# Merge, memory-query and output products of block 2: pairs of column tiles made by Strassen's seven products of quarters

## The chip, the cores and the metric

The kernel runs as one program on one core of a Trainium2 chip. The metric is the device time of one execution in microseconds; the kernel before was timed in three runs. The engines are TensorE (PE, with its weight loads shown as PEld), VectorE (DVE), ScalarE (ACT), GpSimd (POOL) and SyncE (SP, which issues the DMAs).

## The reference

Two blocks of two layers each on 512 tokens of 1024 features, in float32. Block 1 (16 extra tokens in front) mixes windowed attention and an mLSTM. Block 2's layer is the one that the change touches:

```python
h = rmsnorm(x, g_norm)
z = einsum('bsd,dn->bsn', h, w_in)          # 13312 columns, split as
dq, dk, dv, dg, lq, lk, lv, lg, mq, mg, mgate = split(z)
y_a = (rmsnorm(diff_attention(dq, dk, dv)) * (1 - lam_init) * silu(dg)) @ w_br_diff
y_b = (dilated attention of three groups (lq, lk, lv) * silu(lg)) @ w_br_dil
y_m = (memory_attention(mq, keys, values of mem) * silu(mg)) @ w_br_mem
merged = sum over 3 branches of sigmoid(mgate[i]) * (y_a, y_b, y_m)[i]
x = x + merged @ w_out
```

## The kernel before

Activations lie with features on the 128 partitions and the 512 tokens along the free axis: eight tiles of 128 features are one operand. Float32 accuracy is had from three passes: each operand is split into a high and a low part, both float32r (`split`, lines 170 to 174: ACT casts the high part, DVE subtracts it from the source), and `dense` (line 189) adds high·high, high·low and low·high. One dense product of 1024 features by 128 columns is thus 24 matmuls of 512 columns, all into one PSUM bank.

Weights come by DMA in chunks of 128 × 1024 words on SP's queue (`weights`, line 176; tiles `wr`, two buffers), and are split into `wh` and `wl` (three buffers each); of every third chunk POOL makes the low part (line 184), of the others DVE (line 171).

A layer of block 2 (`layer2`) goes in this order: 8 differential heads, 4 dilated heads, then keys and values of the memory (`mem_kv`), 4 memory heads (a dense product for the query and one for the gate each), the merge, and the output projection. The merge has two parts: in part 0 each of 8 column tiles gets one gate product and one product with `w_br_diff`; in part 1 two gate products and two half products with `w_br_dil` and `w_br_mem`. `proj` (line 1206) evacuates a product with a multiplication by the token's norm. Line 1301 makes tanh of a gate, line 1308 multiplies by it, line 1310 (POOL) adds to the sum `acc`, which is then split by line 174. The output projection is eight dense products; line 1327 adds the residual, and `nxt` prepares the next layer's input (parts on lines 173 and 174, squares on 254 and 255).

Attention work is written as generators that move on by a stage whenever `step` is called after a dense product, so that its instructions stand between the products. Intermediate tiles are taken first in, first out from 70 slots in SBUF; a slot's next writer waits for its last reader. The final order on each engine is made by the framework's list scheduler when the program is built; each engine then works through its own list in order. The evacuation of a product is given 300 instructions of precedence (`AHEAD`).

## Time and profile before

| | |
|---|---|
| timed runs, median of 3 | 2871.14 us (2870.21 to 2872.12) |
| the profiled execution: span from first to last instruction | 2868.8 us |
| PE busy in it | 2776.6 us, 97% |
| DVE, ACT, POOL busy | 68%, 49%, 25% |
| mean granted TensorE clock | 0.989 of 2.4 GHz |

The page shows one execution; its 2868.8 us are 2.3 us below the runs' median, so a sum made in its trace carries over to the runs by adding about that. Busy time of an instruction includes the time in which it has started and is held up. PE's durations overlap (a matmul's row is longer than its distance from the next), so PE's pace is read from starts.

### The profile page before, as it was taken

Reading aid. Unit: us, or ns where it says so; the run is one execution under the profiler, and the core shown is the slowest. Engines: PE = TensorE matmul, PEld = TensorE weight load, DVE = VectorE, ACT = ScalarE, POOL = GpSimd, SP = SyncE. Lnnn points to the kernel's source line nnn. Section 1 sums busy time; section 2 is a strip of 40 time slices with the busy share of each in tenths; the row PEclk is TensorE's granted clock in tenths of the full one; section 3 lists DMA queues with packets and bytes.
Section 4 is the critical chain, followed back from the end, with each engine's and each line's share of the span. In section 5 each row is a group of like instructions: output and inputs, shape, how many; then the busy total and the mean of one; then the engine's idle time right before and its main releaser. Section 6 shows DMA issues by size and latency. Waiting matters only on the chain.

```text
span 2868.8 us, 43625 instructions
## 1 busy us (share of the span) xinstructions
PE 2776.6 (97%) x16728; PEld 2446.4 (85%) x16728; DVE 1964.4 (68%) x4261; ACT 1398.6 (49%) x2649; POOL 728.2 (25%) x610
## 2 busy tenths in 40 slices
PE   7999999999999999999999999999998999999997
PEld 7999989999998878878898888888887888888886
DVE  6999886589889757778555772445777664674344
ACT  5555654556565445556443452234555543453223
POOL 5143322224323232221211211322221121211222
PEclk9999999999999999999999999999999999999998
DMA  3221213311111342222223312243221222322232
GB/s 133 67 67 60 67 54 106 116 67 67 61 66 67 113 133 87 80 72 86 89 68 100 122 67 96 99 137 109 80 79 65 87 88 77 110 91 79 96 125 74
DMA packets 96911, 251.60 MB, mean 88 GB/s; under 512 B 9374, under 2 KB 33638, under 8 KB 96574
## 3 DMA queue, kind: packets, MB, share of 16 engines
q1 hardware_dynamic: 96702, 248.82, 26.3%
q8 instruction: 131, 2.15, 0.3%
q14 instruction: 78, 0.64, 0.1%
HBM read 240.19 MB, written 8.60 MB: 87 GB/s over the span
## 4 chain that ended last, share of the span: by engine, by line
PE 75%; DVE 17%; ACT 4%; issue 2%; DMA 1%; SPq 0%; POOL 0%; DVEq 0%; ACTq 0%; POOLq 0%
PE z L164 54%; PE a L164 18%; DVE s L171 2%; DVE wl L171 2%; PE a L943 1%; PE a L486 1%; DVE s L413 1%; DVE s L458 1%; DVE s L329 1%; DVE s L174 1%; DVE s L478 1%; DVE s L276 1%; DVE s L957 1%; DVE s L990 1%; ACT s L470 1%
## 5 line engine op out<-in xcount | busy, mean ns | idle before, releaser
L164 PE MATMUL z<-s,wh 128*128 128x512 f32 (+2 forms) x6784 | 1268.7, 335 | 25.9 <-ACT s L173 9.7
L164 PEld LDWEIGHTS z<-s,wh 128*128 128x128 f32 x6784 | 1045.9, 190 | 159.9 <-ACT s L173 10.3
L164 PE MATMUL z<-s,wl 128*128 128x264 f32 (+2 forms) x3392 | 661.8, 333 | 0.0
L184 POOL TENSOR_TENSOR wl<-wr,wh 128x1024 fp32r<-128x1024 f32 x135 | 333.6, 2471 | 1246.9 <-PE z L164 623.7
L164 PEld LDWEIGHTS z<-s,wl 128*128 128x128 f32 x3392 | 526.5, 188 | 62.4
L170 ACT CAST wh<-wr 128x1024 fp32r<-128x1024 f32 x269 | 281.7, 1048 | 425.5 <-PE z L164 277.8
L164 PE MATMUL a<-s,s 128*128 128x512 f32 (+5 forms) x1900 | 426.6, 339 | 13.9 <-DVE t L458 8.0
L171 DVE TENSOR_TENSOR wl<-wr,wh 128x1024 fp32r<-128x1024 f32 x269 | 354.7, 1321 | 36.9 <-ACT wh L170 32.7
L164 PEld LDWEIGHTS a<-s,s 128*128 128x128 f32 (+1 forms) x1900 | 298.9, 188 | 50.8 <-DVE t L458 9.1
L1206 DVE TENSOR_TENSOR s<-z,s 128x512 f32<-128x512 f32 x128 | 88.0, 688 | 239.9 <-PE z L164 230.3
L183 ACT CAST wh<-wr 128x1024 fp32r<-128x1024 f32 x135 | 141.4, 1048 | 205.0 <-PE z L164 97.1
L171 DVE TENSOR_TENSOR s<-s,s 128x512 fp32r<-128x512 f32 (+6 forms) x272 | 211.7, 789 | 27.4 <-ACT s L170 24.4
L170 ACT CAST s<-s 128x512 fp32r<-128x512 f32 (+6 forms) x272 | 151.1, 567 | 140.3 <-DVE s L1208 26.5
L164 PE MATMUL z<-wh,s 128*128 128x256 f32 x1408 | 208.1, 286 | 5.4 <-DVE s L174 5.0
L164 PEld LDWEIGHTS z<-wh,s 128*128 128x128 f32 x1408 | 188.2, 192 | 14.5 <-DVE s L174 8.1
L171 DVE TENSOR_TENSOR s<-a,s 128x512 fp32r<-128x512 f32 (+3 forms) x266 | 149.8, 581 | 61.2 <-ACT s L170 60.2
L164 PE MATMUL a<-s,wh 128*128 128x512 f32 x768 | 188.2, 393 | 0.0
L170 ACT CAST s<-a 128x512 fp32r<-128x512 f32 (+3 forms) x266 | 127.2, 504 | 93.2 <-PE a L943 49.9
L164 PEld LDWEIGHTS a<-s,wh 128*128 128x128 f32 x768 | 144.0, 188 | 33.4
L957 DVE CUSTOM_DVE_ANT_0 s<-a,reg 128x512 f32<-128x512 f32 x160 | 107.4, 684 | 31.4 <-PE a L164 30.2
L986 ACT ACTIVATE s<-s,t 128x512 f32<-128x512 f32 x128 | 91.3, 715 | 56.7 <-DVE t L983 51.9
L164 PE MATMUL z<-wl,s 128*128 128x256 f32 x704 | 116.9, 284 | 0.0
(254 smaller groups left out, 3068.8 us busy)
## 6 DMA issues: line engine op xcount, KB each, us to landing
wr<-w SPq DMA_DIRECT2D x308, 512.0 KB, 3.5
wr<-wo SPq DMA_DIRECT2D x48, 512.0 KB, 3.4
wr<-wb SPq DMA_DIRECT2D x32, 512.0 KB, 3.5
reg<-tab SPq DMA_DIRECT2D x24, 448.0 KB, 3.5
s<-x SPq DMA_DIRECT2D x16, 264.0 KB, 4.1
r<-s SPq DMA_DIRECT2D x16, 256.0 KB, 2.0
wr<-wmk SPq DMA_DIRECT2D x8, 512.0 KB, 3.4
wr<-wmv SPq DMA_DIRECT2D x8, 512.0 KB, 3.9
```

The source lines that it names most:

```text
L164: self.nc.tensor.matmul(out, lhsT, rhs, start=start, stop=stop)
L170: nc.scalar.copy(hi, src)
L171: nc.vector.tensor_tensor(lo, src, hi.bitcast(F32), ALU.subtract)
L174: nc.vector.scalar_tensor_tensor(lo, src, scale, hi.bitcast(F32), ALU.mult, ALU.subtract)
L183: self.nc.scalar.copy(hi, raw)
L184: self.nc.gpsimd.tensor_tensor(lo, raw, hi.bitcast(F32), ALU.subtract)
L276: nc.vector.scalar_tensor_tensor(z[:, :T], th[:, :T], 1.0, z[:, :T], ALU.add, ALU.mult)
L329: self.nc.vector.tensor_tensor(two(z), ps[:, :, : u - t], two(r), ALU.mult)
L413: nc.vector.tensor_tensor(t[b], z[a], t[a].bitcast(F32), ALU.subtract)
L957: self.nc.vector.tensor_tensor_reduce(e, ps, bias[:, 3 - i : 7 - i].rearrange("p a b -> p (a b)"), 1.0, LOW, ALU.add, ALU.max, mx)
L986: nc.scalar.activation(es[m], es[m], AF.Exp, bias=mx[:, m : m + 1], accum_out=den[:, m : m + 1])
L1206: nc.vector.tensor_tensor(z[:, :512], ps, r[:, :512], ALU.mult)
```

## The change

Columns of two neighbouring tiles (128 + 128 columns of the weights, two halves of 512 features) and two halves of 256 tokens make a product of two-by-two quarters. Instead of eight products of quarters seven are made, after Strassen in Winograd's form: four sums of the weights' quarters (`quarters`, line 220, on POOL), four differences of the activations' quarters (`forms`, line 242) and seven sums of the results (`dense2`, line 265), some of which are made by letting a second product add to a PSUM bank that has been read already. A product of quarters is 12 matmuls of 256 columns, so a pair of tiles has 84 matmuls of 256 columns where it had 48 of 512. Of each layer 20 pairs are made so: the memory heads' query and gate (4), the merge's gates (4 in part 0, 8 in part 1) and the output projection (4).

For the first two uses the activations are read again from the residual in memory, multiplied by gain and norm (line 1408), and their forms are made on POOL, during `mem_kv`; tile k stands with tile k + 4. For the output projection the forms of `acc` are made on DVE, two of four before the last pair of merge tiles and two after it. `mem_kv` now lets the attention units move on between its products. A pair's weights take four `wh` and four `wl` tiles and two `ws` tiles for the sums. Buffers: `wr` 3, `ws` 2, `wh` and `wl` 4 in block 2, for which the weight pool is closed and opened anew between the blocks; 73 slots in block 1, 66 in block 2.

```diff
-NSLOT = 70
+NSLOT, MORE = 66, 7
...
+WBUFS = {"wr": 2, "wh": 3, "wl": 3}, {"wr": 3, "ws": 2, "wh": 4, "wl": 4}
...
+    def second_block(self):
+        assert not any(i >= NSLOT for i, _ in self.held.values())
+        self.idle = deque(i for i in self.idle if i < NSLOT)
+        self.block.close()
+        self.wp = self.pool("wp2")
+        self.wbufs = WBUFS[1]
...
+    def quarters(self, uv):
+        nc = self.nc
+        V, U = self.wtile("wr", F32), self.wtile("wr", F32)
+        nc.sync.dma_start(V, uv[1])
+        nc.sync.dma_start(U, uv[0])
+        S, T = self.wtile("ws", F32), self.wtile("ws", F32)
+        add = lambda o, a, b: nc.gpsimd.tensor_tensor(o, a, b, ALU.add)
+        q = lambda t, i: t[:, 512 * i : 512 * i + 512]
+        parts = lambda: (self.wtile("wh", F32R), self.wtile("wl", F32R))
+        add(q(S, 0), q(U, 0), q(U, 1))
+        add(q(T, 0), q(S, 0), q(V, 0))
+        add(q(S, 1), q(U, 0), q(V, 0))
+        add(q(T, 1), q(T, 0), q(V, 1))
+        v = parts()
+        self.split(V, *v)
+        t, s, u = parts(), parts(), parts()
+        for o, src, i in ((t, T, 0), (s, S, 0), (s, S, 1), (u, U, 1), (t, T, 1)):
+            self.split(q(src, i), q(o[0], i), q(o[1], i))
+        at = lambda p, i: (q(p[0], i), q(p[1], i))
+        return {"11": at(v, 0), "12": at(v, 1), "22": at(u, 1), "1": at(s, 0), "2": at(t, 0), "3": at(s, 1), "4": at(t, 1)}
+    def forms(self, B, a, b, eng):
+        h = lambda t, i: t[:, 256 * i : 256 * i + 256]
+        f, g = self.slot(), self.slot()
+        eng.tensor_tensor(h(f, 0), h(a, 0), h(a, 1), ALU.subtract)
+        eng.tensor_tensor(h(f, 1), h(a, 1), h(b, 1), ALU.subtract)
+        eng.tensor_tensor(h(g, 0), h(b, 1), h(f, 0), ALU.add)
+        eng.tensor_tensor(h(g, 1), h(b, 0), h(g, 0), ALU.subtract)
+        ah = self.rslot()
+        self.split(h(a, 0), h(ah, 0), h(ah, 1))
+        B["11"].append((h(ah, 0), h(ah, 1)))
+        B["slots"].append(ah)
+        for src, k0, k1 in ((b, "21", "22"), (f, "1", "3"), (g, "2", "4")):
+            p = self.pair()
+            self.split(src[:, :512], p[0][:, :512], p[1][:, :512])
+            B["slots"] += p
+            for i, k in enumerate((k0, k1)):
+                B[k].append((h(p[0], i), h(p[1], i)))
+        self.release(f, g)
+    def no_forms(self):
+        return {k: [] for k in ("11", "21", "22", "1", "2", "3", "4", "slots")}
+    def dense2(self, uv, B, bank, first, mid=None):
+        nc, A = self.nc, self.quarters(uv)
+        x, y, z = (bank()[:, :256] for _ in range(3))
+        h = lambda t, i: t[:, 256 * i : 256 * i + 256]
+        u, z1, z2 = self.slot(), self.slot(), self.slot()
+        def product(out, a, b, start):
+            w, n = A[a], len(B[b])
+            seq = [(k, 0, p) for k in range(n) for p in range(2)] + [(k, 1, 0) for k in range(n)]
+            for i, (k, pw, px) in enumerate(seq):
+                nc.tensor.matmul(
+                    out, w[pw][:, 128 * k : 128 * k + 128], B[b][k][px], start=start and i == 0, stop=i == len(seq) - 1, skip_group_check=not start
+                )
+        def tt(o, a, b, op):
+            with self.tc.high_priority(offset=AHEAD):
+                nc.vector.tensor_tensor(o, a, b, op)
+        product(x, "11", "11", True)
+        with self.tc.high_priority(offset=AHEAD):
+            nc.scalar.copy(h(u, 0), x)
+        product(y, "2", "2", True)
+        tt(h(u, 1), h(u, 0), y, ALU.subtract)
+        product(z, "1", "1", True)
+        product(y, "3", "3", False)
+        tt(h(z2, 1), y, h(u, 0), ALU.subtract)
+        tt(h(z2, 1), h(z2, 1), z, ALU.subtract)
+        product(x, "12", "21", False)
+        with self.tc.high_priority(offset=AHEAD):
+            first(h(z1, 0), x)
+        if mid:
+            mid()
+        product(y, "22", "4", False)
+        tt(h(z2, 0), y, h(u, 0), ALU.subtract)
+        product(z, "4", "22", False)
+        tt(h(z1, 1), h(u, 1), z, ALU.add)
+        self.release(u)
+        return z1, z2
...
             mk.append(hl)
+            self.step(RL)
+            if h > 2:
+                next(other)
         mv = []
         for c in range(2):
             v = self.tok2(1)
             self.dense_tok([d["wmv"][l, c, k] for k in range(2)], xs, 2, *v, self.memrc)
             mv.append(v)
+            self.step(RL)
+            next(other)
         self.release(ms)
...
-        mk, mv = self.mem_kv(l)
-        self.step(4)
+        self.release(xs)
+        B = self.no_forms()
+        res = self.res
+        def formed():
+            for m in range(4):
+                t = [self.slot(), self.slot()]
+                for i, k in enumerate((m, m + 4)):
+                    nc.sync.dma_start(t[i][:, :512], res[k, :, :512])
+                    nc.vector.scalar_tensor_tensor(t[i][:, :512], t[i][:, :512], self.col(*gain, k), r[:, :512], ALU.mult, ALU.mult)
+                self.forms(B, *t, nc.gpsimd)
+                self.release(t)
+                yield
+        fs = formed()
+        mk, mv = self.mem_kv(l, fs)
+        for _ in fs:
+            pass
+        self.step(RL)
+        plain = lambda o, ps: nc.scalar.copy(o, ps)
+        step = lambda: self.step(RL)
+        two = lambda: [chunk(), chunk()]
         for h in range(4):
-            q = two_parts(proj())
+            z, g = self.dense2(two(), B, bank, plain, step)
+            q = two_parts(z)
+            self.silu2(g, 512)
             self.step(RL)
-            g = gate(RL)
             db += self.mem_head(h, q, mk, mv, g, yb)
-        acc, mg = [], []
+        def gates():
+            th = lambda o, src: nc.scalar.activation(o, src, AF.Tanh, scale=0.5)
+            z = self.dense2(two(), B, bank, th, step)
+            th(z[1][:, :512], z[1][:, :512])
+            th(z[0][:, 256:512], z[0][:, 256:512])
+            self.step(RL)
+            return z
+        acc, M = [], self.no_forms()
         for part in range(2):
             self.drain((da, db)[part])
             ys = [two_parts(t) for t in (ya, yb)[part]]
-            for m in range(8):
-                gs = []
-                for b in ((0,), (1, 2))[part]:
-                    z = proj()
-                    nc.scalar.activation(z[:, :512], z[:, :512], AF.Tanh, scale=0.5)
-                    gs.append(z)
-                    self.step(RL)
-                w = [self.weights(d["wb2"][l, m, part])]
-                for b, z in enumerate(gs):
-                    ps = self.a()
-                    self.dense([ps], w, ys, FULL, range(8) if part == 0 else range(4 * b, 4 * b + 4))
-                    nc.vector.scalar_tensor_tensor(z[:, :512], z[:, :512], 1.0, ps, ALU.add, ALU.mult)
+            for m2 in range(4):
+                gs = [gates() for _ in range(part + 1)]
+                if part and m2 == 3:
+                    self.release(B["slots"], r)
+                    for k in range(2):
+                        self.forms(M, acc[k], acc[k + 4], nc.vector)
+                        self.release(acc[k], acc[k + 4])
+                for m in (2 * m2, 2 * m2 + 1):
+                    w = [self.weights(d["wb2"][l, m, part])]
+                    for b, z in enumerate(gs):
+                        z = z[m % 2]
+                        ps = self.a()
+                        self.dense([ps], w, ys, FULL, range(8) if part == 0 else range(4 * b, 4 * b + 4))
+                        nc.vector.scalar_tensor_tensor(z[:, :512], z[:, :512], 1.0, ps, ALU.add, ALU.mult)
+                        if part:
+                            nc.gpsimd.tensor_tensor(acc[m][:, :512], acc[m][:, :512], z[:, :512], ALU.add)
+                            self.release(z)
+                        else:
+                            acc.append(z)
                     if part:
-                        nc.gpsimd.tensor_tensor(acc[m][:, :512], acc[m][:, :512], z[:, :512], ALU.add)
-                        self.release(z)
-                    else:
-                        acc.append(z)
-                if part:
-                    p = self.pair()
-                    self.split(acc[m][:, :512], p[0][:, :512], p[1][:, :512], 0.5)
-                    self.release(acc[m])
-                    mg.append(p)
+                        nc.scalar.mul(acc[m][:, :512], acc[m][:, :512], 0.5)
             self.release(ys)
-        self.release(xs, r)
-        res = self.res
-        for m in range(8):
-            ps = self.a()
-            x = self.slot()
-            nc.sync.dma_start(x[:, :512], res[m, :, :512])
-            self.dense([ps], [d["wo2"][l, m]], mg, FULL)
-            nc.vector.tensor_tensor(x[:, :512], x[:, :512], ps, ALU.add)
-            nxt(m, x)
-        self.release(mg)
-    # ------------------------------------------------------------ all of it
+        for k in range(2, 4):
+            self.forms(M, acc[k], acc[k + 4], nc.vector)
+            self.release(acc[k], acc[k + 4])
+        for m2 in range(4):
+            x = [self.slot(), self.slot()]
+            for i in range(2):
+                nc.sync.dma_start(x[i][:, :512], res[2 * m2 + i, :, :512])
+            z = self.dense2(d["wo2"][l, m2], M, bank, plain)
+            for i in range(2):
+                nc.vector.tensor_tensor(x[i][:, :512], x[i][:, :512], z[i][:, :512], ALU.add)
+                self.release(z[i])
+                nxt(2 * m2 + i, x[i])
+        self.release(M["slots"])
...
+        self.second_block()
...
-    nc = bacc.Bacc("TRN2", target_bir_lowering=False, num_devices=1)
+    nc = bacc.Bacc("TRN2", target_bir_lowering=False, num_devices=1, dynamic_dma_scratch_size=1024)
```

In the rows of order below, `s`, `z`, `a`, `wr`, `wh`, `wl`, `ws`, `acc` tiles carry numbers; L246 to L249 are the four differences of `forms`, L227 the sums of weights, L282 the evacuations of `dense2`, L187 the low parts of a split, L1452 and L1470 the former lines 1308 and 1327, L361 the former 255, L190 the former 174.

POOL from the memory's keys to the memory heads, first layer of block 2, before:

```order
L184 TENSOR_TENSOR wl_18760<-wr_18757,wh_18759 128x1024
L184 TENSOR_TENSOR wl_18868<-wr_18865,wh_18867 128x1024
L184 TENSOR_TENSOR wl_18973<-wr_18970,wh_18972 128x1024
L1047 TENSOR_TENSOR s_19037<-s_19037,reg_13687 128x256 x2
L184 TENSOR_TENSOR wl_19198<-wr_19195,wh_19197 128x1024
L1047 TENSOR_TENSOR s_19088<-s_19088,reg_13687 128x256 x2
L184 TENSOR_TENSOR wl_19436<-wr_19433,wh_19435 128x1024
```

and now, from the second `forms` to the fourth (the eight sums of the first two weight pairs stand right ahead):

```order
L247 TENSOR_TENSOR s_19206<-s_19200,s_19201 128x256
L248 TENSOR_TENSOR s_19207<-s_19201,s_19206 128x256
L227 TENSOR_TENSOR ws_19486<-ws_19486,wr_19481 128x512
L246 TENSOR_TENSOR s_19300<-s_19294 128x256
L247 TENSOR_TENSOR s_19300<-s_19294,s_19295 128x256
L249 TENSOR_TENSOR s_19207<-s_19201,s_19207 128x256
L248 TENSOR_TENSOR s_19301<-s_19295,s_19300 128x256
L249 TENSOR_TENSOR s_19301<-s_19295,s_19301 128x256
L246 TENSOR_TENSOR s_19327<-s_19321 128x256
L247 TENSOR_TENSOR s_19327<-s_19321,s_19322 128x256
L248 TENSOR_TENSOR s_19328<-s_19322,s_19327 128x256
L249 TENSOR_TENSOR s_19328<-s_19322,s_19328 128x256
```

POOL had one piece of 1024 in every third chunk there; now sixteen differences stand in front of the third pair's weights, and the last four of them depend on tiles (s_19321, s_19322) that SP loads after the last dilated head's matmuls have freed their slots.

DVE at the end of the merge, first layer, before:

```order
L1206 TENSOR_TENSOR s_21161<-z_21097,s_13765 128x512
L171 TENSOR_TENSOR wl_21294<-wr_21291,wh_21293 128x1024
L1184 TENSOR_TENSOR s_21551<-cols 128x128
L1308 SCALAR_TENSOR_TENSOR s_21161<-s_21161,a_21185 128x512
L1185 TENSOR_REDUCE t_21552<-s_21551 128x2
L1188 TENSOR_SCALAR t_21552<-t_21552 128x1
L174 SCALAR_TENSOR_TENSOR s_21201<-s_20281,s_21200 128x512
L1327 TENSOR_TENSOR s_21205<-s_21205,a_21204 128x512
```

and now (s_20757 and s_20758 are the last two sums `acc`; L187 with `s` are splits of forms):

```order
L1452 SCALAR_TENSOR_TENSOR s_22095<-s_22095,a_22253 128x512
L247 TENSOR_TENSOR s_22327<-s_20371,s_20758 128x256
L248 TENSOR_TENSOR s_22328<-s_20758,s_22327 128x256
L187 TENSOR_TENSOR s_22229<-s_22212,s_22228 128x512
L187 TENSOR_TENSOR s_22337<-s_20758,s_22336 128x512
L249 TENSOR_TENSOR s_22328<-s_20758,s_22328 128x256
L187 TENSOR_TENSOR s_22341<-s_22327,s_22340 128x512
L247 TENSOR_TENSOR s_22306<-s_20370,s_20757 128x256
L248 TENSOR_TENSOR s_22307<-s_20757,s_22306 128x256
L187 TENSOR_TENSOR s_22316<-s_20757,s_22315 128x512
L187 TENSOR_TENSOR s_22345<-s_22328,s_22344 128x512
L249 TENSOR_TENSOR s_22307<-s_20757,s_22307 128x256
```

Before, the last sum's low part (L174) is the only row between the last gate and the residual's first addition; now the differences of two pairs of tiles and their splits stand there.

DVE in the output projection of the first layer, before, two tiles:

```order
L1327 TENSOR_TENSOR s_21331<-s_21331,a_21330 128x512
L171 TENSOR_TENSOR wl_21462<-wr_21459,wh_21461 128x1024
L174 SCALAR_TENSOR_TENSOR s_21366<-s_21331,cols,s_21365 128x512
L255 TENSOR_TENSOR s_21244<-s_21244,s_21369 128x512
L1327 TENSOR_TENSOR s_21373<-s_21373,a_21372 128x512
L174 SCALAR_TENSOR_TENSOR s_21408<-s_21373,cols,s_21407 128x512
```

and now, one pair of tiles:

```order
L187 TENSOR_TENSOR wl_22511<-wr_22500,wh_22510 128x1024
L282 TENSOR_TENSOR s_22386<-s_22386,z_22383 128x256
L187 TENSOR_TENSOR wl_22515<-ws_22505,wh_22514 128x512 x2
L282 TENSOR_TENSOR s_22385<-s_22384,z_22383 128x256
L187 TENSOR_TENSOR wl_22517<-ws_22504,wh_22516 128x512 x2
L1470 TENSOR_TENSOR s_22348<-s_22348,s_22385 128x512
L282 TENSOR_TENSOR s_22386<-z_22382,s_22384 128x256
L187 TENSOR_TENSOR wl_22519<-wr_22501,wh_22518 128x512
L1470 TENSOR_TENSOR s_22349<-s_22349,s_22386 128x512
L190 SCALAR_TENSOR_TENSOR s_22482<-s_22348,cols,s_22481 128x512
L282 TENSOR_TENSOR s_22531<-s_22531,z_22530 128x256
L190 SCALAR_TENSOR_TENSOR s_22490<-s_22349,cols,s_22489 128x512
```

Two tiles had one or two rows of 1024 for weights, two additions, two splits and two sums; a pair now has one row of 1024, five of 512 for weights and five evacuations more.

## Rows read from the trace of the kernel before

**Rows 1.** The page's first part: busy us, share of the span, instructions.

```profile
span 2868.8 us, 43625 instructions
...
PE 2776.6 (97%) x16728; PEld 2446.4 (85%) x16728; DVE 1964.4 (68%) x4261; ACT 1398.6 (49%) x2649; POOL 728.2 (25%) x610
```

**Rows 2.** Windows view by stage, block 2's first layer; the first line names the columns.

```profile
core 0: us, PE busy (x) PEld busy (x) DVE busy (x) ACT busy (x) POOL busy (x), PEclk, DMA share, GB/s
1594.20:1707.90 113.70, 110.15 (x621) 94.58 (x620) 81.90 (x160) 58.41 (x119) 18.85 (x11) 1.00 0.28 94
1707.90:1794.00 86.10, 85.66 (x374) 69.44 (x373) 26.15 (x32) 21.79 (x25) 13.00 (x6) 1.00 0.28 92
1794.00:1916.50 122.50, 122.50 (x531) 99.31 (x530) 56.55 (x55) 35.43 (x44) 38.64 (x23) 1.00 0.32 108
1916.50:1964.00 47.50, 47.50 (x219) 38.97 (x218) 25.22 (x31) 22.12 (x29) 7.59 (x4) 1.00 0.45 154
```

**Rows 3.** Timeline of PE: start, duration (us), instruction, count; 512 columns.

```profile
1732.85 3.86 PE L164 MATMUL z<-s,wh 128*128 128x512 f32 x16
1736.55 2.00 PE L164 MATMUL z<-s,wl 128*128 128x512 f32 x8
1738.39 1.79 PE L164 MATMUL a<-s,wh 128*128 128x512 f32 x7
```

**Rows 4.** Timeline of PE: 256 columns of moving operand, memory keys.

```profile
1594.75 2.05 PE L164 MATMUL z<-s,wh 128*128 128x256 f32 x16
1596.64 1.09 PE L164 MATMUL z<-s,wl 128*128 128x256 f32 x8
1597.57 2.04 PE L164 MATMUL z<-s,wh 128*128 128x256 f32 x16
...
1612.98 2.49 PE L164 MATMUL a<-s,s 128*128 128x512 f32 x14
1616.81 3.52 PE L164 MATMUL z<-s,wh 128*128 128x512 f32 x14 [1.34 <-DVE s L174]
```

**Rows 5.** Timeline of DVE: 512 elements in a chain.

```profile
1685.43 0.68 DVE L171 TENSOR_TENSOR s<-s,s 128x512 fp32r<-128x512 f32 x1
1686.03 0.68 DVE L1119 TENSOR_REDUCE t<-a 128x2 f32<-128x512 f32 x1
1686.63 0.68 DVE L1206 TENSOR_TENSOR s<-z,s 128x512 f32<-128x512 f32 x1
```

**Rows 6.** Timeline of DVE: one instruction of 1024, then of 256.

```profile
1601.22 1.23 DVE L171 TENSOR_TENSOR wl<-wr,wh 128x1024 fp32r<-128x1024 f32 x1 [0.22 <-ACT wh L170]
1602.37 0.42 DVE L171 TENSOR_TENSOR s<-s,s 128x256 fp32r<-128x256 f32 x1
...
1604.36 2.43 DVE L171 TENSOR_TENSOR s<-s,s 128x256 fp32r<-128x256 f32 x1 [0.54 <-ACT s L170]
1606.83 0.69 DVE L957 CUSTOM_DVE_ANT_0 s<-a,reg 128x512 f32<-128x512 f32 x1
...
1613.45 0.42 DVE L1049 TENSOR_REDUCE t<-s 128x1 f32<-128x256 f32 x1
1613.79 0.42 DVE L1048 TENSOR_TENSOR s<-a,s 128x256 f32<-128x256 f32 x1
```

**Rows 7.** Timeline of POOL beside it.

```profile
1604.11 2.40 POOL L184 TENSOR_TENSOR wl<-wr,wh 128x1024 fp32r<-128x1024 f32 x1 [7.50 <-ACT wh L183]
```

**Rows 8.** Groups by form: busy us, mean ns of one, idle before.

```profile
L170 ACT CAST wh<-wr 128x1024 fp32r<-128x1024 f32 x269 | 281.7, 1048 | 425.5 <-PE z L164 277.8 <-PE a L164 47.9 <-DMA wr<-w 41.4
...
L170 ACT CAST s<-s 128x512 fp32r<-128x512 f32 x99 | 60.2, 619 | 60.8 <-DVE s L1208 26.5 <-PE a L164 11.6 <-DVE s L1206 6.7
...
L1310 POOL TENSOR_TENSOR s<-s,s 128x512 f32<-128x512 f32 x32 | 41.3, 1292 | 139.8 <-DVE s L1308 139.8
...
L170 ACT CAST s<-s 128x256 fp32r<-128x256 f32 x49 | 18.2, 403 | 21.3 <-DVE s L1206 13.5 <-DVE s L691 5.0 <-DVE s L1161 2.5
```

**Rows 9.** Line 1047 on POOL: ns min/median/max, 256 elements.

```profile
L1047 POOL TENSOR_TENSOR s<-s,reg x32: 724/746/1782, 1417.0 to 2518.2; 128x256 f32<-128x256 f32 x32
```

**Rows 10.** DMA issues: KB each, us to landing.

```profile
wr<-w SPq DMA_DIRECT2D x308, 512.0 KB, 3.5
...
s<-r SPq DMA_DIRECT2D x16, 256.0 KB, 3.2
```

**Rows 11.** Timeline of PE: the longest wait in block 2.

```profile
1263.99 0.69 PE L943 MATMUL a<-ident,s 128*128 128x128 f32 x2 [4.68 <-DVE s L990]
```

**Rows 12.** Windows around it: busy us of each engine, granted clock, DMA.

```profile
1264.00:1268.00 4.00, 2.73 (x10) 1.82 (x11) 3.55 (x10) 1.40 (x4) 0.00 (x0) 0.50 0.31 108
1268.00:1272.00 4.00, 4.00 (x23) 3.86 (x22) 1.51 (x3) 1.48 (x3) 0.00 (x0) 0.70 0.03 8
```

**Rows 13.** Timeline of PE: the products of the bias tables, between the blocks.

```profile
1052.36 3.27 PE L164 MATMUL a<-s,s 32*20 32x512 f32 x8
```

More of the change, by code (lines that the diff above doesn't have):

```diff
@@ L72, in __init__ @@
         self.pp = pool("pp", space=bass.MemoryType.PSUM)
+        self.block = ExitStack()
+        self.wp = pool("wp", self.block)
+        self.xp = pool("xp", self.block)
+        self.wbufs = WBUFS[0]
         self.n = 0
-        self.idle = deque(range(NSLOT))
+        self.idle, self.below = deque(range(NSLOT + MORE)), NSLOT + MORE
         self.held = {}
@@ L84, in slot @@
     def slot(self, dt=F32, shape=None):
-        i = self.idle.popleft()
-        t = self.sp.tile(shape or [128, L1], dt, name=self.uid("s"), tag=f"s{i}")
+        i = next(i for i in self.idle if i < self.below)
+        self.idle.remove(i)
+        t = (self.sp if i < NSLOT else self.xp).tile(shape or [128, L1], dt, name=self.uid("s"), tag=f"s{i}")
         self.held[id(t)] = (i, t)
@@ L853, in layer1 @@
             self.drain(gens)
+            if l and part:
+                self.below = NSLOT
             ys = []
@@ L1145, in mem_head, with mem_kv @@
         ]
-    def mem_kv(self, l):
+    def mem_kv(self, l, other):
         nc, d = self.nc, self.d
@@ L1170, in mem_kv, with layer2 @@
             mv.append(v)
+            self.step(RL)
+            next(other)
         self.release(ms)
         return mk, mv
-    def layer2(self, l, st, nxt):
+    def layer2(self, l, st, nxt, gain):
         nc, d = self.nc, self.d
@@ L1514, in layout @@
     A["wb2"] = np.stack([[[tile_cols(br[l][p], 128 * m) for p in two] for m in eight] for l in two])
-    A["wo2"] = np.stack([[tile_cols(g["w_out_2"][l], 128 * m) for m in eight] for l in two])
+    A["wo2"] = np.stack([[quarters(g["w_out_2"][l], 256 * m, 256 * m + 128) for m in range(4)] for l in two])
     A["rel_bias"] = np.ascontiguousarray(g["rel_bias_2"])
```

28 lines of the change are left out of this document (17 added, 11 removed).

## The prediction

> **What bounds the kernel now.** I read the page's busy shares first [rows 1]: PE is busy 97% of the span, DVE 68%, ACT 49%, POOL 25%. Then the windows view, cut into stages of block 2's first layer [rows 2]: in part 0, part 1 and the output projection PE is busy for practically the whole stretch, while DVE takes 26 of 86, 57 of 122 and 25 of 47 us. Only from the memory's keys to the first merge multiplication is there idle PE (113.70 − 110.15 = 3.55 us), and there DVE is at 82 of 114, its highest. So columns through PE are the time, and whatever saves columns pays in full, until an engine that makes PE's operands falls behind.
>
> **What is saved.** 24 matmuls of 512 columns start 5.54 us apart, 0.231 each [rows 3]; 24 of 256 columns 2.82 us apart, 0.1173 each [rows 4], so half the columns take 51% of the time. A pair of tiles cost 48 × 0.231 = 11.08 us and will cost 84 × 0.1173 = 9.85: 1.23 less. With 20 pairs in each of two layers: −49 us.
>
> **What DVE and POOL cost each other.** Most of what the change adds has both inputs in SBUF, on DVE (0.60 us for 512 elements [rows 5], 1.13 for 1024, 0.34 for 256 in a chain [rows 6]) or on POOL (0.74 for 256 [rows 9], 1.29 for 512 [rows 8], 2.40 for 1024 [rows 7]). The timeline shows the two don't run side by side: DVE's piece of 256 at 1604.36 took 2.43 us, where the same form took 0.42 at 1602.37, and ended 0.28 after the POOL instruction that had begun 0.25 before it [rows 6, 7]. So I add POOL's time and that of DVE's instructions with two SBUF inputs ("port" below); instructions of DVE that read PSUM, and ACT, are free of it. The Trainium skill ("SBUF — State Buffer", section on the two separate sides) has this as a rule: the shared port pair is an exclusive lock held for a whole instruction, and the loser blocks. This trace agrees (2.43 against 0.42); by it the first stage below costs 47 us of port, and if the two only shared bandwidth it would be DVE's own 35.
>
> **A, memory keys to the first pairs.** Sixteen differences and the first two pairs' eight weight sums fall into the stretch from the first key product to the first three quarter products, as the order shows. Counted there: PE 197 matmuls of 256 columns, 24 transposes (taken alike) and 12 matmuls of 512: 221 × 0.1173 + 12 × 0.231 = 28.7 us. DVE's port: 12 × 0.60 + 8 × 0.34 (splits) + 7 × 0.60 (the scaled reload, line 1408) + 4 × 1.13 + 6 × 0.60 (weights) = 22. DVE's other work there 13, so 35 in all. POOL: 16 × 0.74 + 8 × 1.29 + 2.40 = 24.5. Port together 47, 18 more than PE has; 3.5 of that PE idled already: +15. Bounds: 35 − 28.7 = 6 if nothing blocks; 35 + 24.5 − 28.7 = 31 if nothing overlaps. I take 15, since rows 6 and 7 show full blocking. A chain points the same way: the last two reloads wait on SP's queue for slots that the last dilated head frees, then come 3.2 us of DMA [rows 10], two DVE multiplications, four differences of 0.74, a cast of 0.62 [rows 8] and a low part, 9 to 10 us in series. In the rest of the stage (PE 76 us, port 34 + 28 = 62) the sum fits and only bursts hurt: 3 (0 to 8). A layer 18, both +36 (12 to 78).
>
> **M, end of the merge.** The last gate's quarter comes after the last half product on PE, so behind it stand: evacuation 0.42, tanh 0.40, multiplication 0.68, POOL's addition 1.29, the halving 0.62, three differences of 0.34, a cast 0.62: 5.1 us; the order puts about four splits of 0.60 between: 7.5. PE's own work that doesn't need these tiles is 24 matmuls of 256, 2.8 us. Before, this place had one split and no idle PE [rows 2]. 4.7 a layer, both +9.4 (4.6, without the splits, to 15).
>
> **W, output projection.** Of a layer-0 pair DVE has 1.13 + 5 × 0.60 (weights) + 6 × 0.60 (residual, next input, squares) = 7.7 of port and 5 × 0.34 = 1.7 of evacuations; POOL 4 × 1.29 = 5.2. Port 12.9 against PE's 9.85: +3.0 for each of three pairs (the fourth's sums stand earlier), 9.2; layer 1, without the next layer's parts but with the last norm's, 11.7: 5.6. Together +15. If nothing blocked, DVE's 9.4 would just fit: 0; if evacuations were in series too, 24.
>
> **G, the 24 gate pairs.** Port there is some 27 of 30.8 us for two pairs and two tiles in part 1, less in part 0, and before PE had no idle time there [rows 2]. It is hidden on the whole; bursts +6 (0 to 16, a microsecond for each of part 1's pairs).
>
> **The clock.** The one long wait in block 2, 4.68 us [rows 11], was followed by a granted clock of 0.50 (1.2 GHz) for four microseconds and 0.70 for the next four [rows 12], which costs 4 × 0.5 + 4 × 0.3 = 3.2 us. Four places will have a wait like it (A and M, twice): up to 13; the 1.34 us wait [rows 4] left no such mark, and many small ones may sum up instead, so 7 (0 to 13).
>
> **B and E.** The weight pool is closed between the blocks, so block 2's first chunk loads only when block 1's last product is done: 3.5 us of DMA [rows 10] and a cast of 1.05 [rows 8], against 3.27 us of bias products that need none [rows 13]: +2 (0 to 6). At the end two tiles instead of one are late: +2 (1 to 4). Slots, buffer counts and the smaller descriptor area change no work; their cost, a wait for a slot, is in A's upper bound. Eight reloads of 256 KB a layer go in where DMA is busy at 0.28 [rows 2]: nothing.
>
> **Sum.** −49 + 36 + 9.4 + 15 + 6 + 7 + 2 + 2 = +28. The profiled execution is 2868.8 us, so its span would be 2897; the runs' median lies 2.3 above: **2899 us**.
>
> **Rivals.** *Faster:* POOL's sums mostly fall where DVE reads PSUM or waits, and PE's columns decide. For it: in the merge DVE has over half its time free [rows 2]. Against it: A has too little PE even without blocking. A 6 a layer (12), M 4.6, W and G 0, clock 4, B and E 4: −24, 2847 us. *No change:* half of the blocking bites; A 12 a layer (24), M 9, W 7, clock 5, B and E 4: 49, the gain exactly, 2871 us. *Port as the bound of part 1 too:* every pair of gates brings four weight sums and six weight splits, and if these cluster, each of part 1's 16 pairs loses 1.5 us (24 instead of 6) and A's second stretch 6 instead of 3: +52, 2923 us. It decides from the point where port per two pairs passes PE's 30.8. Against it: the sum of 27. *The seven products aren't cheaper:* if alternating weights in narrow products kept their starts 0.131 apart, 84 would cost the old 11.08: 2948 us. Against it are 24 in 2.82 us, with weights changing every one or two matmuls [rows 4].
>
> **Chances.** Forecast 0.47 (own range 2876 to 2931), faster 0.25, no change 0.12, port in part 1 0.14, no saving 0.02. A measurement of this kernel can tell about 0.2%, 5.7 us, from no change. Slower: 0.47 + 0.14 + 0.02 = 0.63; the same 0.12; faster 0.25. The range 2846 to 2938 takes in the faster case's value, though not its lower half, and most of the part-1 case.
>
> **What the profile after will show.** If I am right: 84 matmuls of 256 columns at 0.117 each; in the first layer's memory stage PE idle of some 15 us in a few waits on DVE or POOL near the four `forms`, and a clock of 0.5 after; DVE busy above 90% in the output projection, its splits of 512 lasting 1.2 to 1.9 us beside POOL's sums; a gap near 5 us ahead of the projection's first products. Wrong is A if PE's idle time there is under 8 us; W if a pair's products start less than 10.5 us apart; the whole of it if DVE's two-input splits keep 0.6 to 0.7 us while POOL runs.

## The result, and the profile after the change

The changed kernel takes 3050.42 us (median of 4 runs, 3044.18 to 3052.06) against 2871.31 for the kernel before: 1.0629 times, interval [1.0616, 1.0641]. The forecast had the sign, with 2899, but 28 us of loss where there are 179, and 3050 lies far above the range. The profiled execution spans 3050.2 us, 181.4 more than that of before. The first part of its page:

```profile
span 3050.2 us, 47632 instructions
...
PE 2821.7 (93%) x18168; PEld 2540.6 (83%) x18168; DVE 2226.3 (73%) x4680; ACT 1521.2 (50%) x2953; POOL 938.6 (31%) x775
```

Against [rows 1], PE's idle time went from 92.2 to 228.5 us, +136.3, and its busy time rose by 45.1, where columns alone should have taken some 45 off it. The pace of narrow products was as forecast: in the timeline of PE (start, duration, instruction, count) twelve matmuls of 256 columns take 12 × 0.118 = 1.42 us (1810.63 to 1812.05; [rows 3, 4] for before), so a pair (84 of them) takes 9.94 us instead of 11.08, and 40 pairs save some 45.

```profile
1810.63 1.11 PE L276 MATMUL z<-s,wh 128*128 128x256 f32 x8
1811.58 0.63 PE L276 MATMUL z<-s,wl 128*128 128x256 f32 x4
1812.05 1.11 PE L276 MATMUL z<-s,wh 128*128 128x256 f32 x8
```

The windows view by the stages of [rows 2] (columns as there; the first window is longer also because attention units now move on inside it, and the lines are, in order, the memory stage, part 0, part 1 and the projection) shows that no stage is free of idle PE any more, and that the granted clock is below 1 in each:

```profile
1605.30:1763.70 158.40, 132.70 (x888) 120.06 (x888) 138.31 (x240) 80.68 (x176) 66.49 (x47) 0.91 0.28 87
1763.70:1854.90 91.20, 85.98 (x531) 77.40 (x530) 50.51 (x67) 34.01 (x56) 28.87 (x18) 0.96 0.28 87
1854.90:1986.80 131.90, 114.75 (x740) 103.81 (x738) 87.08 (x117) 54.11 (x94) 73.80 (x49) 0.97 0.31 93
1986.80:2039.70 52.90, 41.61 (x272) 38.14 (x271) 42.02 (x64) 24.93 (x46) 13.66 (x10) 0.82 0.34 101
```

In part 1 DVE is busy for 87 of 132 us, so it isn't short of time there, and PE still idles for 17. The waits view of PE shows what it waited for most in the products of pairs and beside them (total us, times, longest):

```profile
PE z L276 <- DVE s L282: 51.6, 57, 4.6
PE z L276 <- DVE s L187: 26.4, 14, 5.9
PE z L180 <- DVE s L190: 19.1, 17, 3.2
PE z L276 <- ACT s L186: 11.2, 10, 1.9
```

Line 282 is an evacuation inside a pair: a later product of the pair adds to the bank, or the next pair begins in it, and PE may not start before DVE has read what is there. Three timelines of the same ten microseconds, PE, DVE and POOL, at the first pair of part 1's gates (in the windows above it still lies in the second line, since the third begins with part 1's first merge product):

```profile
1831.23 0.64 PE L276 MATMUL z<-s,wl 128*128 128x256 f32 x4
1833.44 1.18 PE L276 MATMUL z<-s,wh 128*128 128x256 f32 x8 [1.58 <-DVE s L282]
...
1835.87 0.64 PE L276 MATMUL z<-s,wl 128*128 128x256 f32 x4
1838.54 0.62 PE L276 MATMUL z<-s,wh 128*128 128x256 f32 x3 [2.03 <-DVE s L282]
```

```profile
1829.50 3.47 DVE L187 TENSOR_TENSOR s<-s,s 128x512 fp32r<-128x512 f32 x2
1832.89 0.41 DVE L282 TENSOR_TENSOR s<-s,z 128x256 f32<-128x256 f32 x1
1833.22 1.28 DVE L187 TENSOR_TENSOR wl<-ws,wh 128x512 fp32r<-128x512 f32 x2
1834.42 0.67 DVE L1452 SCALAR_TENSOR_TENSOR s<-s,a 128x512 f32<-128x512 f32 x1
1835.02 1.47 DVE L187 TENSOR_TENSOR wl<-wr,wh 128x512 fp32r<-128x512 f32 x1
1836.41 0.67 DVE L1452 SCALAR_TENSOR_TENSOR s<-s,a 128x512 f32<-128x512 f32 x1
1837.01 1.15 DVE L187 TENSOR_TENSOR s<-s,s 128x512 fp32r<-128x512 f32 x1
1838.09 0.41 DVE L282 TENSOR_TENSOR s<-s,z 128x256 f32<-128x256 f32 x1
```

```profile
1829.01 1.73 POOL L227 TENSOR_TENSOR ws<-wr 128x512 f32<-128x512 f32 x1 [3.41 <-DVE s L187]
1830.69 1.73 POOL L227 TENSOR_TENSOR ws<-wr,wr 128x512 f32<-128x512 f32 x1
1834.65 2.97 POOL L227 TENSOR_TENSOR ws<-ws,wr 128x512 f32<-128x512 f32 x2 [2.23 <-DVE wl L187]
```

The evacuation at 1832.89 takes its 0.41 us. It is late because two splits ahead of it in DVE's queue took 3.47 us, beside two of POOL's sums, where two splits at 1833.22, with POOL idle, took 1.28; PE, which is at the pair's second product and needs the bank of the pair before, waits 1.58 us. The next evacuation, at 1838.09, stands behind a split of 1.47 and one of 1.15 beside the other two sums, and PE waits 2.03. What the clock then does, the windows around show (granted clock third from the end): 1.00, then 0.54 (near the lower level, 1.2 GHz) after a few microseconds in which PE was busy 3.01 of 5.

```profile
1833.50:1838.50 5.00, 3.01 (x24) 2.81 (x24) 4.99 (x7) 1.03 (x3) 2.89 (x2) 1.00 0.18 37
1838.50:1845.20 6.70, 6.14 (x29) 5.85 (x30) 2.60 (x5) 2.47 (x4) 0.00 (x0) 0.54 0.26 94
1845.20:1850.20 5.00, 5.00 (x41) 5.00 (x41) 3.24 (x7) 3.09 (x6) 0.00 (x0) 0.93 0.13 51
```

Not every wait on line 282 is a late evacuation. In a pair of part 0 DVE had been idle for about 2 us ahead of each of two (PE, then DVE):

```profile
1791.55 1.21 PE L276 MATMUL z<-s,wh 128*128 128x256 f32 x8 [0.58 <-DVE s L282]
1793.74 1.21 PE L276 MATMUL z<-s,wh 128*128 128x256 f32 x8 [0.52 <-DVE s L282]
```

```profile
1791.07 0.42 DVE L282 TENSOR_TENSOR s<-s,z 128x256 f32<-128x256 f32 x1 [2.06 <-PE z L276]
1793.26 0.42 DVE L282 TENSOR_TENSOR s<-z,s 128x256 f32<-128x256 f32 x1 [1.77 <-PE z L276]
```

Counted in the trace, 37 of the 57 waits are of 0.65 us or less, 18.0 us in all, little more each than the evacuation itself; the other 20 make 33.6 us. In 14 of the 40 pairs, all of them the first, third, fifth and so on, the list scheduler has not kept the order of the program text, as far as the times show it: DVE's first reading of the second bank starts only after the pair's third product, the fourth product starts 0.05 us after that reading, and the fifth 0.05 us after the next one. So the two products into that bank have none between them. The fourth and fifth products of these 14 pairs have 26.4 of the 51.6 us. A pair takes three banks, and `z` (line 126) hands them out two to a tile, so that in every second pair the first two banks are one tile. That the program's dependencies go by the tile, not by the bank, would give this order; that is a reading, and no run takes the two apart.

At the end of the merge four waits of PE follow on one another, and from within the first of them the clock is at half for some 24 us (timeline of PE, then windows):

```profile
1983.60 1.43 PE L276 MATMUL z<-s,wh 128*128 128x256 f32 x5 [5.58 <-DVE s L187]
...
1989.16 0.58 PE L276 MATMUL z<-s,wh 128*128 128x256 f32 x1 [1.72 <-DVE s L187]
1991.68 0.58 PE L276 MATMUL z<-s,wh 128*128 128x256 f32 x1 [1.94 <-ACT s L186]
1993.51 1.01 PE L276 MATMUL z<-s,wh 128*128 128x256 f32 x3 [1.25 <-DVE s L187]
```

```profile
1982.00:1994.00 12.00, 5.50 (x20) 4.62 (x21) 11.92 (x20) 5.97 (x11) 4.06 (x3) 0.52 0.32 89
1994.00:2006.00 12.00, 10.97 (x50) 10.38 (x50) 3.83 (x7) 2.75 (x5) 0.24 (x1) 0.50 0.21 64
```

The sums of a windows view over all stretches at half clock, before and after:

```profile
sum 64.45, PE 41.83 PEld 36.56 DVE 44.74 ACT 22.15 POOL 10.16; mean PE 3.80 PEld 3.32 DVE 4.07 ACT 2.01 POOL 0.92
```

```profile
sum 223.33, PE 162.31 PEld 148.24 DVE 153.87 ACT 91.16 POOL 51.35; mean PE 4.92 PEld 4.49 DVE 4.66 ACT 2.76 POOL 1.56
```

A matmul of 256 columns takes about twice its time there (10.97 us for 50 in the windows just above, 0.22 each instead of 0.118), so an estimate of what the lower clock takes is (162.3 − 41.8) / 2 = 60 us, some 7 of it in block 1. The 181.4 are then: 136 more idle, 60 of lower clock, less 45 of columns saved, and a rest of 30 that was not traced.

### The profile page after: what moved, and what is told of

It is laid out like the page before. It is cut to its first block, busy times and chain, and to the rows that moved or that the text cites. A ratio compares the mean times of both kernels' runs of the same rounds, so it can differ in the third digit from the quotient of the medians.

```text
span 3050.2 us, 47632 instructions
## 1 busy us (share of the span) xinstructions
PE 2821.7 (93%) x18168; PEld 2540.6 (83%) x18168; DVE 2226.3 (73%) x4680; ACT 1521.2 (50%) x2953; POOL 938.6 (31%) x775
## 5 line engine op out<-in xcount | busy, mean ns | idle before, releaser
L180 PE MATMUL z<-s,wh 128*128 128x264 f32 (+2 forms) x5760 | 1031.1, 328 | 33.5 <-ACT s L189 9.4
L180 PEld LDWEIGHTS z<-s,wh 128*128 128x128 f32 x5760 | 865.8, 193 | 128.4 <-DVE s L190 12.3
L186 ACT CAST wh<-wr 128x1024 fp32r<-128x1024 f32 (+1 forms) x296 | 292.6, 989 | 404.7 <-PE z L180 196.9
L276 PE MATMUL z<-s,wh 128*128 128x256 f32 x2240 | 352.8, 301 | 98.0 <-DVE s L282 51.6
L187 DVE TENSOR_TENSOR wl<-wr,wh 128x1024 fp32r<-128x1024 f32 (+1 forms) x296 | 380.0, 1284 | 74.9 <-ACT wh L186 54.2
L276 PEld LDWEIGHTS z<-s,wh 128*128 128x128 f32 x2240 | 312.5, 203 | 124.9 <-DVE s L282 53.6
L187 DVE TENSOR_TENSOR s<-s,s 128x512 fp32r<-128x512 f32 (+4 forms) x336 | 275.4, 836 | 21.4 <-ACT s L186 14.3
L186 ACT CAST s<-s 128x512 fp32r<-128x512 f32 (+4 forms) x336 | 185.3, 567 | 188.3 <-DVE s L1319 37.5
L187 DVE TENSOR_TENSOR s<-a,s 128x512 fp32r<-128x512 f32 (+3 forms) x266 | 149.3, 581 | 73.5 <-ACT s L186 72.2
L276 PE MATMUL z<-s,wl 128*128 128x256 f32 x1120 | 191.4, 295 | 1.3 <-DVE wl L187 1.3
L201 ACT CAST wh<-wr 128x1024 fp32r<-128x1024 f32 x108 | 113.1, 1047 | 133.4 <-PE z L180 81.0
L187 DVE TENSOR_TENSOR wl<-ws,wh 128x512 fp32r<-128x512 f32 x160 | 131.8, 853 | 29.6 <-ACT wh L186 16.8
```

The source lines that it names most:

```text
L180: self.nc.tensor.matmul(out, lhsT, rhs, start=start, stop=stop)
L186: nc.scalar.copy(hi, src)
L187: nc.vector.tensor_tensor(lo, src, hi.bitcast(F32), ALU.subtract)
L201: self.nc.scalar.copy(hi, raw)
L276: nc.tensor.matmul(out, w[pw][:, 128 * k : 128 * k + 128], B[b][k][px], start=start and i == 0, stop=i == len(seq) - 1, skip_group_check=n ...
```

## The experiments

Lengths of stages in the profiled executions, in us. A layer of block 2 is cut at its first product for the attention's values and at its first merge product, so a memory stage holds the attention ahead of it; e1 and the rest are below.

```
                                  before  changed    e1      e4      e9      e6      e13     e17
block 1                           1060.6  1084.6   1064.4  1067.3  1064.5  1066.5  1065.0  1065.6
layer 0, attention and memory      641.2   673.1    675.9   661.1   677.2   679.6   650.7   654.1
layer 0, merge and projection      256.6   293.6    294.9   268.8   276.4   264.5   259.2   252.3
layer 1, attention and memory      638.9   686.0    688.4   671.4   681.0   671.5   658.8   650.3
layer 1, merge, projection, end    271.5   312.9    313.0   280.3   290.6   279.0   271.6   265.1
```

**e1: 70 slots in block 1.** All later kernels but e2 and e12 are made from this one.

```diff
-NSLOT, MORE = 66, 7
+NSLOT, MORE = 66, 4
```

> The changed kernel with 70 slots in block 1 instead of 73, which gives block 1 the same order of instructions as before the change up to its last stage. Theory S (block 1's 24 us of the loss come from the other order that three more slots lead to): block 2 starts near 1063 us instead of 1085 and the time falls by 18 to 24 us, to about 3030. Rival B (they come from the weight pool that is closed and opened anew between the blocks): within 6 us of 3050.

3038.0 us, 1.0581 [1.0564, 1.0599]: 12 us less. Block 1 is 20 us shorter in the profile, within 4 of before; the rest is 7 longer. So three more slots, which change no work in block 1, cost it most of its 24 us; the order of its instructions changed with them.

**e2 and e12: no Strassen product.** Block 2's layer as before the change, in the new weight buffers; in e12 with four slots less in the attention. One line of the edit, which puts the whole layer back:

```diff
-        mk, mv = self.mem_kv(l, fs)
+        mk, mv = self.mem_kv(l)
```

> No Strassen product at all: block 2's layer as before the change (plain products, mem_kv as before), but in the changed kernel's weight buffers (three wr, four wh and wl) with the weight pool opened anew between the blocks; 70 slots. Theory W (what block 2 lost comes from the seven products and what they need): 2865 to 2876 us, as before. Rival B (the deeper buffers or the new pool reorder the attention to its harm): 2885 to 2900, with the first layer's attention 6 and the second's 20 us longer, as in the changed kernel.

> e2 (no Strassen product, 2878 us) with only 66 of the 70 slots given out from the start of block 2's layer to the memory's keys. Theory S (four slots less make the attention of block 2 longer, 552 and 563 us in e1 against 540 and 551 in e2): 15 to 25 us above e2, about 2898. Rival (that difference comes from the preparation of the pairs that begins before the memory's values): within 5 us of e2.

2877.97 us, 1.0027 [1.0015, 1.0039], and 2874.82, 1.0019 [1.0010, 1.0028]. The two theories of harm by buffers or slots fall, but for 5 to 8 us: block 2's loss comes with the seven products and what they need.

**e4 and e8: the sums of weights.** e4 leaves the four sums out; in e8 POOL makes them and nothing reads them. The edit of e4, with the four `add` lines taken out besides, then that of e8:

```diff
-        S, T = self.wtile("ws", F32), self.wtile("ws", F32)
+        S, T = U, V
```

```diff
-        for o, src, i in ((t, T, 0), (s, S, 0), (s, S, 1), (u, U, 1), (t, T, 1)):
+        for o, src, i in ((t, V, 0), (s, U, 0), (s, U, 1), (u, U, 1), (t, V, 1)):
```

> e1 without the four sums of the weights' quarters on POOL: the splits read the quarters as they come, all else is kept (this leaves a part of the computation out). Theory P (POOL's sums hold up DVE's instructions with two SBUF inputs, and these hold up PE): 80 us or more below e1, about 2945, with DVE's splits of 512 weights at 0.68 instead of 0.85 us and few waits left on line 282. Theory L (latency of the evacuations in a pair): 10 to 30 us below e1, about 3010, since the chain of evacuations stays.

> e1 (3038 us) with POOL's four sums of weights made as before, but read by nothing: the splits take the quarters as they come (a part of the computation is left out by it). e4, without the sums, took 2951. Theory P (the port: a sum holds up DVE's instructions with two SBUF inputs, whoever needs it): most of the 87 us stay, 3000 to 3035, DVE's splits of 512 weights at 0.8 us or more. Rival C (the chain: DMA, four dependent sums, cast, split, and PE late for each pair): the sums cost little when nobody waits for them, 2950 to 2970.

2950.69 us, 1.0284 [1.0268, 1.0299], and 3027.56, 1.0542 [1.0518, 1.0566]: 87 and 10 us below e1. So 77 of the 87 us stay when nobody needs the results: the harm is mostly in the sums' running. DVE shows it: first the page's line of e1 and that of e4, then the group of splits of 512 weights in e4 and that in e8 (count, busy us, mean ns).

```profile
PE 2810.3 (93%) x18168; PEld 2531.2 (83%) x18168; DVE 2231.4 (73%) x4680; ACT 1517.2 (50%) x2953; POOL 936.1 (31%) x775
```

```profile
PE 2773.7 (94%) x18168; PEld 2506.2 (85%) x18168; DVE 2134.6 (72%) x4680; ACT 1516.7 (51%) x2953; POOL 691.6 (23%) x615
```

```profile
L187 DVE TENSOR_TENSOR wl<-wr,wh 128x512 fp32r<-128x512 f32 x200 | 131.7, 685 | 5.5 <-ACT wh L186 4.0 <-PE z L272 1.5
```

```profile
L187 DVE TENSOR_TENSOR wl<-wr,wh 128x512 fp32r<-128x512 f32 x200 | 167.5, 863 | 6.4 <-PE z L276 4.5 <-ACT wh L186 1.7
```

The same 4680 instructions of DVE are busy 97 us less without the sums; a split of 512 weights takes 685 ns without them and 863 beside them. PE's waits on the evacuations in e1 and in e4 (where they are line 278) say the same:

```profile
PE z L276 <- DVE s L282: 51.4, 55, 4.5
```

```profile
PE z L272 <- DVE s L278: 23.3, 38, 1.3
```

The long ones are gone. Of the 23.3 us that are left, 17.9 are at the fourth and fifth product of the same 14 pairs as above, in 28 waits: POOL doesn't cause those.

**e9: the sums on DVE.**

```diff
-        add = lambda o, a, b: nc.gpsimd.tensor_tensor(o, a, b, ALU.add)
+        add = lambda o, a, b: nc.vector.tensor_tensor(o, a, b, ALU.add)
```

> e1 with the four sums of weights on DVE instead of POOL; everything is computed. DVE gets 160 instructions of 512 more, 160 x 0.60 = 96 us, and POOL loses 245 us. Theory P (POOL's long hold on the port is the harm): DVE's total busy time stays near 2230, since the new work takes the place of the time held up, and the run is 20 to 50 us faster than e1, about 3000. Rival D (DVE's own throughput bounds these stages): as slow as e1 or slower, 3035 to 3080.

2989.98 us, 1.0416 [1.0398, 1.0434], 48 below e1. DVE takes on 160 instructions and is busy as long as before them:

```profile
PE 2791.1 (93%) x18168; PEld 2514.6 (84%) x18168; DVE 2234.3 (75%) x4840; ACT 1516.9 (51%) x2953; POOL 700.3 (23%) x615
```

**e3: the order of the products.** The products that add to the first and third bank come between those that use the second (cuts in the code are marked; two sums of results change places with them).

```diff
-        product(y, "3", "3", False)
         ...
         product(x, "12", "21", False)
+        product(y, "3", "3", False)
         ...
-        product(y, "22", "4", False)
         product(z, "4", "22", False)
+        product(y, "22", "4", False)
```

> e1 with another order of the seven products: two products instead of one between the first use of the second bank and its second use, and the third bank read before the second is added to. Theory L (PE waits for the evacuation of a bank that it has to add to, with only one product of 1.4 us in between): PE's waits on line 282, 52 us in the changed kernel, fall below 25, the clock is lowered less often, and the time falls by 35 to 70 us against e1, to about 2975. Rival P (DVE and POOL don't get their work done in time, whatever the order): the waits move to other lines and the time stays within 15 us of e1.

3011.53 us, 1.0491 [1.0472, 1.0510], 26 below e1, between the two theories' values. The waits on line 282 fell from 51.4 to 33.6 us, not below 25.

**e5: no differences on POOL.** In `forms` the four differences are skipped where `eng` is POOL.

> e1 without the sixteen differences a layer that POOL makes for the memory and gate products (the halves themselves are split instead; a part of the computation is left out). POOL loses 32 x 0.75 = 24 us. Theory P (POOL's burst with DVE's splits makes the memory stage late): the stage falls from 124 to about 112 us in each layer, the time by 20 to 30 us, to about 3013. Rival R (reloading the residual, its multiplication and the 28 splits set the stage): under 8 us, 3030 or more.

3020.67 us, 1.0520 [1.0491, 1.0548], 17 below e1. Attention and memory together lost 6.6 and 9.0 us (669.3 and 679.4), about half of what theory P said for the stage; the time lies between theory P's 20 to 30 and the rival's 8.

**e6 and e16: the projection.** e6 makes it of plain products; e16 pairs tile 2k with 2k + 1, so that one group of differences stands behind the last merge tile instead of two. Of e16's edit:

```diff
-                    for k in range(2):
-                        self.forms(M, acc[k], acc[k + 4], nc.vector)
+                    for k in range(3):
+                        self.forms(M, acc[2 * k], acc[2 * k + 1], nc.vector)
```

> e1 with the output projection as before the change (eight plain products a layer, no differences of the merged sum); the memory heads and gates keep the seven products. PE has 8 x 1.23 = 10 us more of columns. Theory E (the end of the merge and the projection, where DVE has most to do, lose about 30 us a layer by idle PE and low clock): 40 to 55 us below e1, about 2990. Rival G (the gates lose most): at most 20 below e1, 3020 or more.

> e1 (3038 us) with the output projection's tiles paired as 2k with 2k + 1 instead of k with k + 4 (the weights' rows laid out to match), so that three of the four groups of differences are made before the last pair of merge tiles and one after it. Theory M (PE waits at the projection's start for the differences, splits and evacuations behind the last merge tile): its 10 us of idle a layer halve, and some of the 24 us at half clock that follow go, 12 to 30 us below e1, about 3018. Rival (DVE is behind in the projection anyway, the waits come later): within 8 us of e1.

e6: 2961.33 us, 1.0314 [1.0297, 1.0332], 77 below e1, though PE has 9 us more of columns: eight pairs lost 86, their saved columns not counted. In the table 30 and 34 us of it lie in merge and projection, and 17 in layer 1's attention and memory, which start from layer 0's results; that they had waited for these is likely, and not isolated. e16: 3031.33, 1.0564 [1.0545, 1.0583], 7 below e1 by medians (their intervals overlap): the rival's 8 us hold, and the differences behind the last tile are the lesser part.

**e10, e11 and e14: what helped, together.** e10 is e1 with e3, e9 and e6; e11 makes POOL's differences on DVE too; e14 is e11 with a fourth bank for each pair, so that in the program text two products stand between any two uses of a bank.

> e1 with the three changes that helped: the order of e3 (-26 us), the sums of weights on DVE (e9, -48) and the plain projection (e6, -77); everything is computed. If they were independent 3038 - 151 = 2887; part of the first two lies in the projection that the third takes away (18 + 22 of e9's 48 us were won between the merge's start and the layers' ends), so 2895 to 2920 is expected. Rival (what is left after the port is relieved is hidden, and 32 pairs pay 1.23 us each): below 2866, faster than before the change.

> e10 with the sixteen differences of a layer on DVE instead of POOL: 32 x 0.34 = 11 us more for DVE, 24 us less for POOL. Theory P (port): 5 to 15 us below e10, both memory stages some 5 us shorter. Rival R (reloads and splits set the memory stage, DVE is its bound): within 4 us of e10 or slower.

> e11 (2931 us) with a fourth bank for the third product instead of adding it to the second's bank, so that at least two products stand between the uses of a bank; the same number of evacuations, everything computed. Theory L (PE waits for evacuations of a bank it has to use again): the 24 us of waits on line 282 go, and with them some low clock: 25 to 45 us below e11, about 2896. Rival P (DVE's work as such is late): within 10 us of e11.

2937.90, 2931.28 and 2940.95 us: 1.0234 [1.0217, 1.0251], 1.0216 [1.0201, 1.0231], 1.0246 [1.0225, 1.0266]. The gains overlap by a third (100 of 151), POOL's remaining differences cost 7 by medians (the intervals overlap), the fourth bank brought nothing: waits on line 282 were 24.2 us in e11 and 36.3 in e14. With four banks the first and second bank are one tile in every pair, so e14 doesn't tell what a fourth bank of its own would do. None is near the kernel before.

**e13, e15 and e17: seven products with nothing to prepare.** All sums and differences of weights and activations are left out, in the order of e3; e15 adds the fourth bank with e14's order, e17 takes the projection out.

> e3 with all 40 pairs as seven products and their evacuations, but none of the sums and differences of weights and activations: each pair's two chunks and each pair of tiles are split as for plain products, and the seven products take these quarters (that part of the computation is left out). Theory P (DVE's and POOL's preparation is what loses the time, the columns are saved in full): 3038 less some 200 us, 2835 to 2855. Rival L (the chain of evacuations inside a pair keeps PE waiting even with DVE at leisure): 2875 or more.

> e13 (2906 us; the seven products without sums and differences, a part of the computation left out) with the fourth bank as in e14. Theory L: 19 us of waits on the evacuations go with what follows on them, 20 to 40 us below e13, 2866 to 2886. Rival (the loss in e13 lies outside the pairs, in the next layer's late input and in the memory stage's order): within 10 us of e13.

> e13 (2906 us; seven products without sums and differences, a part of the computation left out) with the projection as before the change, so 32 pairs in the memory heads and gates. Theory J (what e13 loses lies at the projection: its results come late, and the next layer's attention, 564 us in e13 against 546 in e6, waits for them): 20 to 45 us below e13, 2861 to 2886, at or below the kernel before. Rival G (heads and gates themselves don't gain, whatever feeds them): within 10 us of e13, or 2895 and more.

2906.37, 2906.74 and 2881.96 us: 1.0127 [1.0112, 1.0142], 1.0119 [1.0102, 1.0136], 1.0037 [1.0023, 1.0051]. Theory P's words that the columns are saved in full are refuted: even free of these sums, 40 pairs lose 1.3%, 36 to 39 us. The fourth bank cut the waits on the evacuations (line 264 there) from 18.8 to 11.2 us and nothing of the time, so theory L doesn't explain the loss. 24 us of it lay at the projection (theory J): without it layer 1's attention and memory are 8.5 us shorter, each stage of merge and projection 7. In e17 merge and projection are 4 and 6 us below before, where twelve gate pairs should give 14. And e2, with plain products in the same weight buffers, takes 2877.97 us: against it the 32 pairs of e17 gain nothing (the intervals of the two ratios overlap), where 36 us of columns are saved.

## Why the prediction was wrong

Right were the sign, the pace of narrow products (45 us saved for 49), the two engines' holding each other up, and the boundary (block 1 of e1 ends 4 us later than before; 2, up to 6, were given). As the Trainium skill has it ("SBUF — State Buffer", section on the two separate sides), a DVE instruction with two SBUF inputs and a GpSimd one that reads SBUF block each other: the trace agrees, the splits went to 863 ns beside sums that nobody needed (e8), and evacuations that read PSUM stayed at 0.41 us. Of the signs named, the gap ahead of the projection (5.58 us) and a granted clock near 0.5 behind it came, and idle time in the memory stage (25.7 us in its window); DVE above 90% in the projection did not: 42.0 of 52.9 us, 79%.

The step that failed is in **G** and **W**: "It is hidden on the whole; bursts +6". I set DVE's and POOL's sums of time over a stage against PE's, and where the sum was smaller I called it hidden. But PE waits for single evacuations with one product of 1.42 us in between, in 14 pairs none, and these stand in DVE's queue behind splits that a sum of 1.3 to 1.7 us holds up. A stage with a third of DVE's time free still lost 17 us of PE. For **G**'s 6 the runs show some 43: in e6, with a plain projection, merge and projection are 7.9 and 7.5 us longer than before, where twelve gate pairs a layer should have made them 14 shorter. The forecast did not list as waits the products that add to a bank already read, though the change adds four to each pair; e3 shows that another order of them is worth 26 us. For the projection with the merge's end (**W**, **M**) I had 15 + 9; e6 shows 86. Both figures have the clock's part in them.

**The clock** was 7 and is 60 by the estimate above. I priced four places with a wait of 4 us and more, and put short ones in the same 7; the rows at 1838 show the level fall after waits of 1.58 and 2.03 us a few microseconds apart.

**A** was 36. The table gives +32 for layer 0, and +47 − 17 (e6) for layer 1; with 5 each of saved columns that is about 72, near the upper bound of 78. POOL's sums weigh more in it than its differences: e4 takes 15 to 17 us off each layer's stage, e5 only 7 to 9. With block 1's 24 and the 45 saved, 43 + 86 + 72 + 24 − 45 = 180 accounts for the loss; the terms come from different runs, so that they meet so closely is in part luck.

**Slots and order**, "no work" and so no cost of their own, were 12 us of the runs' time (e1). That the unchanged block 1 would be ordered anew could have been read from the order of the two kernels.

The rivals: port as the bound of part 1 too, 2923, was nearest in mechanism, but the bound is not port time per pair of tiles, since DVE has idle time there. No saving, 2948, was nearest in time, and the pace of the products refutes it. The faster rival is refuted by e13: even with the preparation gone the columns didn't decide.

Left open is why pairs free of sums and differences don't pay. e17 has 36 us of columns less and is no faster than before or than e2; PE idles for 123 us in its profile, 92 before and 97 in e2, and its attention and memory stages are 13 and 11 us longer than before, but no run isolates the cause. Nor does one separate what the waits cost by themselves from what the lower clock behind them adds.

## What to carry to other kernels

Where PE never idles, fewer columns pay only if everything that PE waits for keeps its distance. Count the waits that a scheme adds per product and ask what stands ahead of the releasing instruction in its engine's queue; a stage's busy share doesn't answer that. Look in the trace, too, whether the products run in the order of the program text. Work for GpSimd isn't free beside VectorE's two-input instructions: moving the weights' sums to VectorE itself won 48 us here. And price a cluster of short waits by the granted clock behind it.

## What was not expected of the hardware

Sums on POOL are held up as DVE is: a sum of 512 elements, 1.29 us in the mean before the change [rows 8], took 1.73 at 1829.01 and a mean of 1442 to 1640 ns by form in e1. The clock stayed at half for 24 us at the merge's end, with PE busy for 10.97 of the last 12.
